# mLSTM scores over all 128 rows, and layer 0's modulation chunks moved off the mLSTM's weights

## The chip, the core and the metric

The kernel runs on one core of a Trainium2 chip. The metric is the device time of one execution in microseconds (us). A core has five engines that run their own instruction streams and wait for each other through semaphores: TensorE (PE; its weight loads are PEld), VectorE (DVE), ScalarE (ACT), GpSimd (POOL) and SyncE (SP), which issues the DMA transfers here.

## What is computed

The reference is a trunk of two layers over 256 latent and 256 context tokens of width 1024, in fp32. Each layer has four mixers side by side, a gated merge, an output projection and an MLP. Two pieces of it matter here. The modulation vector of a layer is a matrix product of one row, which the kernel forms in chunks of weights:

```python
mod = jnp.split((s_c @ w_ada[l] + b_ada[l])[:, None, :], 6, axis=-1)
mod_c = jnp.split(s_cc @ w_ada[l][:, :n_cm * D_MODEL] + b_ada[l][:n_cm * D_MODEL], n_cm)
...
x_l = x_l + mod[2] * (merge_branches((ya_l, yb_l, yc_l, yd_l), lat['gates'], w_branch[l]) @ w_out[l])
```

The mLSTM mixer (B) has 4 heads with keys and queries of 64 columns and values of 128. For each head and each of two directions it computes

```python
s = jnp.einsum('bhtk,bhsk->bhts', qc, kc) * jnp.exp(dmat - m_t[..., None])
num = w_inter[..., None] * jnp.einsum('bhtk,bhkv->bhtv', qc, cmat) + jnp.einsum('bhts,bhsv->bhtv', s, vc)
den = w_inter * jnp.einsum('bhtk,bhk->bht', qc, nvec) + jnp.sum(s, axis=-1)
```

## The kernel before

**Weights.** Every large product is split into a high and a low half of fp32: three products for one. A weight tile is 128x1024 (512 KB). SyncE loads it into one of three `raw` buffers (`_prep`), ScalarE copies its high half `whi` (L139), VectorE subtracts to get the low half `wlo` (L140), and TensorE then runs 24 products of 512 columns with it. Weights are prepared one ahead of use. `plan` writes the list of loads (`specs`) in the order of use; `get` takes the next.

**Modulation chunks.** `plan` puts one chunk of `w_ada` behind each planned weight as long as the list `fill` has any. For layer 0 the list has four halves of eight chunks (`ada_specs`, groups g1 and g2, halves 0 and 1). A chunk is 128x1024, goes through the same `raw` buffers and costs two VectorE updates of an accumulator `aacc` (`ada_chunk`, L390 for a half's first chunk and L392 for the others), one for the latent and one for the context vector. When a half is complete, `ada_sum` sums it over the partitions: eight TensorE products with 32 columns of weights (L404) into a tile of the pool `pm`, a ScalarE copy to a row tile `arow` of the pool `d2` (L407), two transposes (L263) and two VectorE additions into `mod` (L414). `ada_chunk` notes from which use on the sum may be made (`pending`); `get` makes it when that point is reached.

**Order of the work.** A string of units sets in which order the program is written; for layer 0 it is "A RA B b b M0 b b b b b b M0 M0 CD M0 RB C ...". A and RA are the first mixer and its readout; B is the mLSTM's projections (kv, bk, bq, bv: 12 weights) and state; each b is one mLSTM head (four context heads, then four latent ones); each M0 is a quarter of the merge of the first mixer (two gate weights, one branch weight); CD the projections of the two attentions; RB the mLSTM's readout (bo: 4 weights); C the attention. A scheduler then orders the instructions of each engine, in which the heads fall between the products of the weights. Accumulators of weights come from the pool `pd` (4 tiles), those of everything else on TensorE from `pm` (4). A merge quarter's two gate tiles in `pd` are read by two tanh on ScalarE (L1231), which go to `d2` tiles (3).

**A head** (`mixer_b`, from L867). Its scores are two fp32 products of 64 rows and 256 columns (L873). Then for each of the two directions: a product that broadcasts a row of maxima (L878), two VectorE sums with limits (L884, L887), an exponential on ScalarE (L889), two VectorE products with the scores (L890, L891), for latent heads the decayed query `qw` (memset L896, exponential L897, product L898), and five products with the values and the state (L908). At the end the denominator (L912 to L914) and the normalised sum (L917 on ScalarE, L918 on VectorE).

Of the kernel before, what the change touches and what calls it, by code (L numbers as in the profile page):

```python
# [10 lines left out]
AF = mybir.ActivationFunctionType  # L11
# [7 lines left out]
KT = DM // 128  # L19
# [21 lines left out]
class Trunk:  # L41
# [53 lines left out]
    def plan(self, key, parts, split=True, dest=None, fill=True):  # L95
        self.specs.append((key, parts, split, dest))
        if fill and split and self.fill:
            self.specs.append(self.fill.pop(0))

    def wide(self):  # L100

# [268 lines left out]
    def ada_specs(self, l, g):  # L370
        w = self.io["w_ada"]
        out = []
        for k in range(KT):
            for j in range(2):
                c0 = g * 2048 + j * 1024
                out.append((("ada", l, g, k, j), [(w[l, k * 128:(k + 1) * 128, c0:c0 + 1024].rearrange("p (a c) -> p a c", a=1), (1, 1024))], False, None))
        return sorted(out, key=lambda o: o[0][4])

    def ada_chunk(self, key):

        nc = self.nc
        _, l, g, k, jj = key
        raw, _ = self.get(key)
        sides = (0, 1) if l == 0 or g == 0 else (0,)
        if k == 0:
            self.ada_acc = [self.t("w4", [128, 1024], name=f"aacc{g}{jj}{r}") for r in sides]
        for r in sides:
            acc, s = self.ada_acc[r], self.scol[:, k, r:r + 1]
            if k == 0:
                nc.vector.tensor_scalar(out=acc, in0=raw, scalar1=s, scalar2=None, op0=ALU.mult)  # L390
            else:
                nc.vector.scalar_tensor_tensor(out=acc, in0=raw, scalar=s, in1=acc, op0=ALU.mult, op1=ALU.add)  # L392
        if k == KT - 1:
            self.pending = (l, g, jj, sides, self.ada_acc, self.next_use + 1)

    def ada_sum(self, now=False):
        nc = self.nc
# [362 lines left out]
    def mixer_b(self, l):  # L760
        nc = self.nc
# [3 lines left out]
        sides = ((0, 0), (1, CTX)) if need else ((1, CTX),)  # L765
# [26 lines left out]
        for a in range(2):  # L792
            o = a * 256
# [28 lines left out]
        kT = [self.conv(l, 1, mt, self.fm(self.get(("bk", l, mt)), 0, TOK), 0, 0.125) for mt in range(2)]  # L822
        qT = [self.conv(l, 0, mt, self.fm(self.get(("bq", l, mt)), q0, TOK), q0, 1.0) for mt in range(2)]
# [43 lines left out]
        for (sd, t0) in sides:  # L867
            for h in range(HEADS):
                pns = []
                mt, p0 = h // 2, (h % 2) * 64  # L870
                pS = self.pm()
                for st in range(2):
                    nc.tensor.matmul(pS[:, st * 256:(st + 1) * 256], kT[mt][p0:p0 + 64, t0 + st * 128:t0 + (st + 1) * 128],  # L873
                                     qT[mt][p0:p0 + 64, t0:t0 + 256], start=True, stop=True, skip_group_check=True)
                for d in range(2):
                    row = d * 32 + h
                    pM = self.pm()
                    nc.tensor.matmul(pM[:, 0:256], self.rsel[0:100, row:row + 1].to_broadcast([100, 128]), nM[0:100, t0:t0 + 256],  # L878
                                     start=True, stop=True)
                    E = self.t("w2", [128, 512])[:, 0:384]  # L880
                    full = d
                    part = 1 - d
                    tile_of = lambda st: 2 * sd + st
                    nc.vector.scalar_tensor_tensor(out=E[:, 0:256], in0=pM[:, 0:256], scalar=U[:, tile_of(full), row:row + 1],  # L884
                                                   in1=self.mfull[d], op0=ALU.add, op1=ALU.min)
                    pt = slice(128, 256) if d == 0 else slice(0, 128)
                    nc.vector.scalar_tensor_tensor(out=E[:, 256:384], in0=pM[:, pt], scalar=U[:, tile_of(part), row:row + 1],  # L887
                                                   in1=(self.mskf if d == 0 else self.mskb), op0=ALU.add, op1=ALU.min)
                    nc.scalar.activation(out=E, in_=E, func=AF.Exp)  # L889
                    nc.vector.tensor_tensor(out=E[:, 0:256], in0=E[:, 0:256], in1=pS[:, full * 256:(full + 1) * 256], op=ALU.mult)  # L890
                    nc.vector.tensor_tensor(out=E[:, 256:384], in0=E[:, 256:384],  # L891
                                            in1=pS[:, part * 256 + pt.start:part * 256 + pt.stop], op=ALU.mult)
                    if sd:

                        qw = self.t("w2", [128, 512])[:, 0:256]
                        nc.gpsimd.memset(qw[64 - p0:128 - p0], 0.0)  # L896
                        nc.scalar.activation(out=qw[p0:p0 + 64], in_=pM[p0:p0 + 64, 0:256], func=AF.Exp, bias=ME[p0:p0 + 64, 1, row:row + 1])  # L897
                        nc.vector.tensor_tensor(out=qw[p0:p0 + 64], in0=qw[p0:p0 + 64], in1=qT[mt][p0:p0 + 64, t0:t0 + 256], op=ALU.mult)  # L898
                    pn = self.pm()
                    for tt in range(2):  # L900
                        o = pn[:, tt * 129:(tt + 1) * 129]
                        srcs = [(E[:, tt * 128:(tt + 1) * 128], V[:, tile_of(full), h, :])]
                        if tt == (1 if d == 0 else 0):
                            srcs.append((E[:, 256:384], V[:, tile_of(part), h, :]))
                        if sd:
                            srcs.append((qw[:, tt * 128:(tt + 1) * 128], C[:, d, mt, :]))
                        for n, (a, b) in enumerate(srcs):
                            nc.tensor.matmul(o, a, b, start=(n == 0), stop=(n == len(srcs) - 1), skip_group_check=True)  # L908
                    pns.append(pn)
                den = self.sm([128, 2, 2], "bden", 4)  # L910
                for d in range(2):
                    nc.scalar.activation(out=den[:, d, :], in_=pns[d][:, 0:258].rearrange("p (a b) -> p a b", a=2)[:, :, 128], func=AF.Abs)  # L912
                nc.vector.tensor_tensor(out=den, in0=den, in1=EM[:, 2 * sd:2 * sd + 2, :].rearrange("p a b -> p b a")[:, h:h + 33:32, :], op=ALU.max)
                nc.vector.reciprocal(out=den, in_=den)  # L914
                for tt in range(2):
                    o = H[:, 2 * sd + tt, h * 128:(h + 1) * 128]
                    nc.scalar.activation(out=o, in_=pns[0][:, tt * 129:tt * 129 + 128], func=AF.Copy, scale=den[:, 0, tt:tt + 1])  # L917
                    nc.vector.scalar_tensor_tensor(out=o, in0=pns[1][:, tt * 129:tt * 129 + 128], scalar=den[:, 1, tt:tt + 1], in1=o,  # L918
                                                   op0=ALU.mult, op1=ALU.add)
                yield  # L920
# [114 lines left out]
    def mixer_c(self, l):  # L1035
        nc = self.nc
        need = l == 0
        i0 = 0 if need else 2
        q0 = i0 * 128
        KVD, QS, R = self.KVD, self.QS, self.CDR  # L1040
        kn = self.t("w2", [128, 4, 128], name=f"ckn{l}")
        for i in range(4):
            kv = kn[:, i, :].rearrange("p (h c) -> p h c", h=2)
# [323 lines left out]
    def run(self):  # L1367
        nc = self.nc
        for l in range(2):
            if l == 0:  # L1370
                self.plan_start()
                self.fill += self.ada_specs(0, 1) + self.ada_specs(0, 2)
            m = [0] * 4
            for u in ORDER[l].split():
                if u == "A":
                    self.plan_a(l)
                elif u == "RA":
                    self.plan_tmw(("ag", l), l, O_AG)
                elif u == "B":
                    self.plan_b(l)  # L1380
                elif u == "CD":
                    self.plan_cd(l)
                elif u == "RB":
                    self.plan_tmw(("bo", l), l, O_BO)
                elif u[0] == "M":
                    r = int(u[1])
                    self.plan_merge(l, r, (m[r],))
                    m[r] += 1
            self.plan_out(l)
            if l == 0:  # L1390
                self.fill += self.ada_specs(1, 0) + self.ada_specs(1, 1) + self.ada_specs(1, 2)
            self.plan_ff(l)
# [60 lines left out]
        for i in range(2):  # L1453
            for h in range(2):
                o = self.ot[i][:, h * 512:(h + 1) * 512]
# [73 lines left out]
```

## Time and profile before

| | us |
|---|---|
| median of 3 runs | 1815.01 (1813.83 to 1816.32) |
| the profiled execution, its own time | 1811.02 |
| its span, first to last instruction | 1809.2 |
| TensorE busy | 1766.8 |
| VectorE busy | 1201.0 |
| ScalarE busy | 834.5 |
| GpSimd busy | 121.6 |

The profile is one execution. Busy times are sums of instructions; matmuls are pipelined, so the start-to-start step of two products is what each costs in a row, and the printed duration of one is longer than that. Times in the rows below are counted from the start of the span.

### The profile page before, as it was taken

The page shows a single profiled execution, that of the slowest core. Times are in us where ns is not written, and L with a number is a line of the kernel's source. Part 1 is how long each engine was busy: PE and PEld are TensorE (multiplying, and loading weights), DVE is VectorE, ACT ScalarE, POOL GpSimd, SP SyncE. Part 2 cuts the span into 40 slices and gives each one's busy share as a digit, 9 for nine tenths or more (in the row PEclk, how much of TensorE's full clock was granted, in tenths as well). Part 3 has the DMA queues.
Part 4 walks back from the last instruction along what each step waited for, and adds up shares of the span by engine and source line. Part 5 has one row for each costly group of instructions (what it writes and reads, how often), then busy time and mean ns, then how long its engine had stood idle before and what let it go on. Part 6 is the DMA issues. An engine that isn't in the chain of part 4 may idle for free.

```text
span 1809.2 us, 26349 instructions
## 1 busy us (share of the span) xinstructions
PE 1766.8 (98%) x10214; PEld 1494.7 (83%) x10214; DVE 1201.0 (66%) x2047; ACT 834.5 (46%) x1481; POOL 121.6 (7%) x139
## 2 busy tenths in 40 slices
PE   7999989999999999999999999999999999999998
PEld 5788867888677778898888888888789779989998
DVE  5798998657744435489884435587666965656665
ACT  4443533455753334343333334443465664545555
POOL 0000000000011101020101010000000001001110
PEclk9999999999999999999999999999999999999999
DMA  9643345232022234337783334222345425445554
GB/s 294 204 122 102 115 143 162 68 103 84 30 59 70 70 128 128 94 129 222 260 274 93 93 94 140 77 73 57 94 118 179 129 70 162 147 134 164 185 180 137
DMA packets 210045, 234.71 MB, mean 130 GB/s; under 512 B 8320, under 2 KB 186880, under 8 KB 209664
## 3 DMA queue, kind: packets, MB, share of 16 engines
q1 hardware_dynamic: 209920, 233.03, 42.7%
q8 instruction: 80, 1.31, 0.3%
q14 instruction: 45, 0.37, 0.1%
HBM read 228.80 MB, written 4.19 MB: 129 GB/s over the span
## 4 chain that ended last, share of the span: by engine, by line
PE 86%; DVE 6%; ACT 3%; DMA 2%; issue 2%; SPq 0%; POOL 0%; ACTq 0%; DVEq 0%; POOLq 0%
PE pd L198 15%; PE pd L196 15%; PE pd L197 15%; PE pd L168 4%; PE pd L167 4%; PE pd L169 4%; PE pd L238 4%; PE pd L240 4%; PE pd L239 4%; PE pm L263 3%; PE pm L636 2%; DVE wlo L140 2%; PE pm L908 1%; PE pm L1094 1%; DMA raw<-in_w_in_dram 1%
## 5 line engine op out<-in xcount | busy, mean ns | idle before, releaser
L140 DVE TENSOR_TENSOR wlo<-raw,whi 128x1024 fp32r<-128x1024 f32 (+1 forms) x305 | 384.7, 1261 | 278.5 <-ACT whi L139 276.5
L139 ACT ACTIVATE whi<-raw 128x1024 fp32r<-128x1024 f32 (+1 forms) x305 | 321.7, 1056 | 407.4 <-PE pd L197 184.3
L198 PE MATMUL pd<-HH,wlo 128*128 128x256 f32 (+1 forms) x1104 | 371.5, 337 | 2.0 <-DVE wlo L140 1.8
L196 PE MATMUL pd<-HH,whi 128*128 128x256 f32 (+1 forms) x1104 | 372.4, 337 | 0.0
L197 PE MATMUL pd<-HL,whi 128*128 128x256 f32 (+1 forms) x1104 | 370.5, 336 | 0.0
L198 PEld LDWEIGHTS pd<-HH,wlo 128*128 128x128 f32 x1104 | 209.5, 190 | 24.3 <-DVE wlo L140 4.0
L196 PEld LDWEIGHTS pd<-HH,whi 128*128 128x128 f32 x1104 | 209.8, 190 | 21.9 <-issue 1.5
L197 PEld LDWEIGHTS pd<-HL,whi 128*128 128x128 f32 x1104 | 209.8, 190 | 20.3 <-issue 0.5
L196 PE MATMUL pd<-b,whi 128*128 128x256 f32 (+1 forms) x528 | 175.8, 333 | 0.0
L198 PE MATMUL pd<-b,wlo 128*128 128x256 f32 (+1 forms) x528 | 175.4, 332 | 0.2 <-DVE wlo L140 0.2
L197 PE MATMUL pd<-b,whi 128*128 128x256 f32 (+1 forms) x528 | 175.6, 333 | 0.0
L196 PEld LDWEIGHTS pd<-b,whi 128*128 128x128 f32 x528 | 100.4, 190 | 10.5 <-issue 0.8
L198 PEld LDWEIGHTS pd<-b,wlo 128*128 128x128 f32 x528 | 100.4, 190 | 10.2 <-DVE wlo L140 1.0
L238 PE MATMUL pd<-whi,HH 128*128 128x512 f32 (+1 forms) x272 | 106.9, 394 | 1.3 <-ACT whi L139 1.0
L197 PEld LDWEIGHTS pd<-b,whi 128*128 128x128 f32 x528 | 100.4, 190 | 9.4 <-DVE b L1355 0.2
L239 PE MATMUL pd<-whi,HL 128*128 128x512 f32 (+1 forms) x272 | 106.0, 390 | 0.0
L240 PE MATMUL pd<-wlo,HH 128*128 128x512 f32 (+1 forms) x272 | 105.0, 390 | 0.0
L169 PE MATMUL pd<-HH,wlo 128*128 128x512 f32 (+1 forms) x232 | 88.9, 383 | 7.2 <-DVE wlo L140 7.2
L434 ACT ACTIVATE w<-X 128x256 f32<-128x256 f32 x120 | 47.5, 412 | 104.7 <-DVE X L1251 104.7
L1244 POOL TENSOR_TENSOR mg<-mg,d 128x512 f32<-128x512 f32 (+1 forms) x48 | 53.1, 1108 | 555.7 <-DVE d L1243 540.8
L1354 POOL TENSOR_TENSOR d<-d 128x256 f32<-128x256 f32 (+1 forms) x60 | 56.0, 938 | 492.0 <-ACT b L1352 477.1
L168 PE MATMUL pd<-HL,whi 128*128 128x512 f32 (+1 forms) x232 | 89.0, 384 | 0.0
(425 smaller groups left out, 3302.8 us busy)
## 6 DMA issues: line engine op xcount, KB each, us to landing
raw<-in_w_in_dram SPq DMA_DIRECT2D x140, 512.0 KB, 3.7
raw<-in_w_ff_dram SPq DMA_DIRECT2D x128, 512.0 KB, 3.6
w<-in_w_ada_dram SPq DMA_DIRECT2D x48, 512.0 KB, 4.9
raw<-in_w_ada_dram SPq DMA_DIRECT2D x32, 512.0 KB, 3.8
raw<-in_w_branch_dram SPq DMA_DIRECT2D x24, 512.0 KB, 3.5
raw<-in_w_out_dram SPq DMA_DIRECT2D x16, 512.0 KB, 3.5
w<-in_w_ada_dram SPq DMA_DIRECT2D x28, 256.0 KB, 5.6
raw<-in_w_branch_dram SPq DMA_DIRECT2D x16, 256.0 KB, 4.0
```

Source lines behind the costliest of these rows:

```text
L139: nc.scalar.activation(out=hi[:, 0:n], in_=raw[:, 0:n], func=AF.Copy)
L140: nc.vector.tensor_tensor(out=lo[:, 0:n], in0=raw[:, 0:n], in1=hi[:, 0:n].bitcast(F32), op=ALU.subtract)
L167: nc.tensor.matmul(out, lh, rh, start=(i == 0), stop=False)
L168: nc.tensor.matmul(out, lh, rl, start=False, stop=False)
L169: nc.tensor.matmul(out, ll, rh, start=False, stop=(i == n - 1))
L196: nc.tensor.matmul(o, wh, act[0], start=(k == 0), stop=False, skip_group_check=True)
L197: nc.tensor.matmul(o, wh, act[1], start=False, stop=False, skip_group_check=True)
L198: nc.tensor.matmul(o, wl, act[0], start=False, stop=(k == KT - 1), skip_group_check=True)
L238: nc.tensor.matmul(o, hh, wh, start=(k == 0), stop=False, skip_group_check=True)
L239: nc.tensor.matmul(o, hl, wh, start=False, stop=False, skip_group_check=True)
L240: nc.tensor.matmul(o, hh, wl, start=False, stop=(k == KT - 1), skip_group_check=True)
L1354: eng.tensor_tensor(out=r, in0=r, in1=r, op=ALU.mult)
```

## The change

1. A head's scores take the queries from a new tile `qz` of 128 rows, the head's 64 rows copied by ScalarE and the other 64 zeroed by GpSimd, so that the two products have 128 rows (both heads of the key tile stand in the other operand).
2. While B's weights are planned, `fill` is empty: no chunk stands behind them. For layer 0 the list of chunks has an empty entry after each half, so that one weight between two halves has none. The same 32 chunks are used; the last twelve fall behind later weights, up to the last weight of RB.
3. The sum of a half of layer 0 may be made one use earlier (`next_use + l`), and is made at the latest before the next half's first chunk and at the start of the attention C. For layer 1 the number is as before; there, too, the sum now comes at the latest with the next half's first chunk.

```diff
     def plan(self, key, parts, split=True, dest=None, fill=True):
         self.specs.append((key, parts, split, dest))
         if fill and split and self.fill:
-            self.specs.append(self.fill.pop(0))
+            spec = self.fill.pop(0)
+            if spec is not None:
+                self.specs.append(spec)
...
-        return sorted(out, key=lambda o: o[0][4])
+        out = sorted(out, key=lambda o: o[0][4])
+
+        return out if l else out[0:KT] + [None] + out[KT:] + [None]
...
         if k == 0:
+            self.ada_sum(True)
...
-            self.pending = (l, g, jj, sides, self.ada_acc, self.next_use + 1)
+            self.pending = (l, g, jj, sides, self.ada_acc, self.next_use + l)
...
+                qz = self.t("w2", [128, 512])[:, 0:256]
+                nc.gpsimd.memset(qz[64 - p0:128 - p0], 0.0)
+                nc.scalar.activation(out=qz[p0:p0 + 64], in_=qT[mt][p0:p0 + 64, t0:t0 + 256], func=AF.Copy)
                 pS = self.pm()
                 for st in range(2):
-                    nc.tensor.matmul(pS[:, st * 256:(st + 1) * 256], kT[mt][p0:p0 + 64, t0 + st * 128:t0 + (st + 1) * 128],
-                                     qT[mt][p0:p0 + 64, t0:t0 + 256], start=True, stop=True, skip_group_check=True)
+                    nc.tensor.matmul(pS[:, st * 256:(st + 1) * 256], kT[mt][:, t0 + st * 128:t0 + (st + 1) * 128],
+                                     qz, start=True, stop=True, skip_group_check=True)
...
         KVD, QS, R = self.KVD, self.QS, self.CDR
+        self.ada_sum(True)
...
                 elif u == "B":
+
+                    keep, self.fill = self.fill, []
                     self.plan_b(l)
+                    self.fill = keep
```

The scheduler gives another order, too. Line numbers of the changed kernel are larger by 2 to 10: L882 there is the score product (L873 before), L887 the broadcast (L878), L898 and L906 the exponentials (L889, L897), L917 the products with values and state (L908), L921 and L926 the denominator and the normalised half (L912, L917), L409, L412 and L265 the sum, its row and the transposes (L404, L407, L263), L1241 the tanh (L1231), L198 a gate product (L196), L142 a low half (L140), L397 a chunk's update (L392). `pm_...`, `pd_...` and `w2_...` are tiles of the pools.

On TensorE, from the end of the second latent head's products to the third head's in the changed kernel:

```order
L917 MATMUL pm_307_2581<-C0_2197,w2_306_2577 128x129
L882 MATMUL pm_310_2599<-w2_309_2596,w2_218_1960 128x256
L887 MATMUL pm_311_2602<-nM0_1883,rsel_101 128x256
L917 MATMUL pm_314_2614<-bv0_2062,w2_312_2604 128x129
L887 MATMUL pm_315_2620<-nM0_1883,rsel_101 128x256
L917 MATMUL pm_314_2614<-C0_2197,w2_313_2610 128x129
```

The next head's broadcast and its first direction's products follow at once. The same place before, after the second direction of a latent head:

```order
L908 MATMUL pm_311_2651<-C0_2285,w2_310_2647 128x129
L873 MATMUL pm_313_2666<-w2_229_2092,w2_223_2006 128x256
L878 MATMUL pm_314_2669<-nM0_1905,rsel_101 128x256
L198 MATMUL pd_340_2875<-HH_125,wlo87_2881 128x512
L196 MATMUL pd_340_2875<-HH_125,whi87_2880 128x512
L197 MATMUL pd_340_2875<-HL_126,whi87_2880 128x512
```

Here products of a gate weight (`wlo87`, `whi87`) follow the broadcast; seven of them and then twelve of the next weight stand before the head's first direction goes on. In the changed kernel none stands from the second latent head's first direction to the end of the fourth head.

On TensorE of the changed kernel, where those heads end (`aacc110` and `aacc111` are a half's two accumulators, `arow011` its row, `whi71` a gate weight of the third merge quarter):

```order
L917 MATMUL pm_329_2683<-C0_2197,w2_328_2679 128x129
L409 MATMUL pm_333_2734<-aacc110_1539,selr_97 32x256 x3
L409 MATMUL pm_333_2734<-aacc111_1540,selr_97 32x256 x4
L265 MATMUL pm_335_2745<-cst_75,arow011_2743 128x128 x2
L198 MATMUL pd_342_2824<-HH_125,whi71_2788 128x512
```

The sum's products and the transposes of its row stand ahead of the next weight's products.

On ScalarE of the changed kernel at the same place (`d2_336` and `d2_337` are the tanh of the gate tiles of the second merge quarter):

```order
L906 ACTIVATE w2_328_2679<-pm_326_2671,bME_227_2048 64x256
L921 ACTIVATE bden_330_2689<-pm_325_2665 128x2
L921 ACTIVATE bden_330_2689<-pm_329_2683 128x2
L412 ACTIVATE arow011_2743<-pm_333_2734 128x256
L1241 ACTIVATE d2_336_2780<-pd_331_2698 128x512
L1241 ACTIVATE d2_337_2782<-pd_332_2699 128x512
L926 ACTIVATE bh0_2224<-pm_325_2665,bden_330_2689 128x128 x2
```

And before, around one of the same quarter's two tanh (`d2_341`):

```order
L139 ACTIVATE whi88_2912<-raw88_2910 128x1024
L889 ACTIVATE w2_305_2623<-w2_305_2623 128x384
L897 ACTIVATE w2_306_2629<-pm_304_2621,bME_232_2102 64x256
L1231 ACTIVATE d2_341_2940<-pd_339_2874 128x512
L889 ACTIVATE w2_309_2641<-w2_309_2641 128x384
L897 ACTIVATE w2_310_2647<-pm_308_2639,bME_232_2102 64x256
```

The tanh stood between the exponentials of a head; now they stand behind the row of the sum, which stands behind the last head's exponentials.

On VectorE of the changed kernel, between the low halves of two of RB's weights (98 and 100), where the attention's queries `qs0` are prepared:

```order
L142 TENSOR_TENSOR wlo98_3433<-raw98_3430,whi98_3432 128x1024
L397 SCALAR_TENSOR_TENSOR aacc211_3163<-raw99_3462,scol_112,aacc211_3163 128x1024
L1064 TENSOR_TENSOR qs0_2936<-qs0_2936,cdr_382_3270 128x512 x2
L1066 TENSOR_TENSOR qs0_2936<-qs0_2936,gain_651 128x512
L939 TENSOR_TENSOR w2_412_3616<-qs0_2936,rt_659 128x16x16
L142 TENSOR_TENSOR wlo100_3467<-raw100_3464,whi100_3466 128x1024
```

And before, between low halves 99 and 100:

```order
L140 TENSOR_TENSOR wlo99_3407<-raw99_3404,whi99_3406 128x1024
L1056 TENSOR_TENSOR qs0_2996<-qs0_2996,gain_651 128x512
L930 TENSOR_TENSOR w2_404_3592<-qs0_2996,rt_659 128x16x16 x2
L932 TENSOR_TENSOR w2_403_3591<-qs0_2996,rt_659 128x512
L1054 TENSOR_TENSOR qs0_2996<-qs0_2996,cdr_377_3292 128x512
L933 TENSOR_TENSOR w2_403_3591<-w2_403_3591,w2_404_3592 128x512
L930 TENSOR_TENSOR w2_406_3600<-qs0_2996,rt_659 128x16x16
L1060 COPY qs0_2996<-w2_403_3591 128x512
L930 TENSOR_TENSOR w2_406_3600<-qs0_2996,rt_659 128x16x16
L932 TENSOR_TENSOR w2_405_3599<-qs0_2996,rt_659 128x512
L140 TENSOR_TENSOR wlo100_3437<-raw100_3434,whi100_3436 128x1024
```

Chunk updates now share this stretch with the preparation of the attention.

## Rows read from the trace of the kernel before

**Rows 1.** The page's busy times: us, share of the span, number of instructions.

```profile
PE 1766.8 (98%) x10214; PEld 1494.7 (83%) x10214; DVE 1201.0 (66%) x2047; ACT 834.5 (46%) x1481; POOL 121.6 (7%) x139
```

**Rows 2.** Windows: length, busy us (instructions) by engine, granted TensorE clock, DMA share, GB/s.

```profile
220.00:240.00 20.00, 17.14 (x86) 12.88 (x85) 18.01 (x29) 11.24 (x14) 0.00 (x0) 1.00 0.51 152
240.00:260.00 20.00, 17.22 (x70) 13.33 (x69) 18.40 (x27) 7.11 (x12) 0.00 (x0) 0.91 0.40 109
260.00:280.00 20.00, 19.65 (x101) 15.23 (x99) 16.54 (x22) 6.57 (x9) 0.00 (x0) 1.00 0.77 238
...
380.00:400.00 20.00, 20.00 (x135) 18.50 (x134) 9.05 (x14) 13.32 (x31) 0.00 (x0) 1.00 0.27 80
400.00:410.00 10.00, 10.00 (x46) 8.29 (x45) 10.00 (x27) 3.13 (x4) 0.00 (x0) 1.00 0.38 105
410.00:420.00 10.00, 10.00 (x46) 8.29 (x45) 9.05 (x23) 2.12 (x2) 0.00 (x0) 1.00 0.38 107
420.00:430.00 10.00, 10.00 (x47) 8.21 (x46) 4.28 (x5) 3.23 (x5) 0.00 (x0) 1.00 0.36 105
```

**Rows 3.** TensorE's waits, 205 to 282 us: total us, times, longest.

```profile
PE pd L169 <- DVE wlo L140: 4.6, 2, 2.9
```

**Rows 4.** Groups of VectorE lines, 205 to 282 us: busy us, mean ns | idle before.

```profile
L392 DVE SCALAR_TENSOR_TENSOR aacc<-raw,scol,aacc 128x1024 f32<-128x1024 f32 x19 | 23.9, 1274 | 0.0
L140 DVE TENSOR_TENSOR wlo<-raw,whi 128x1024 fp32r<-128x1024 f32 (+1 forms) x12 | 14.4, 1200 | 4.9 <-ACT whi L139 4.8
```

**Rows 5.** Timeline of TensorE, latent heads and attention: start us, us, instruction, records.

```profile
340.45 0.61 PE L908 MATMUL pm<-bv,w 128*128 128x129 f32 x4
...
340.99 0.70 PE L873 MATMUL pm<-w,w 64*128 64x256 f32 x2
...
348.57 0.61 PE L908 MATMUL pm<-bv,w 128*128 128x129 f32 x4
349.02 0.39 PE L908 MATMUL pm<-C,w 128*128 128x129 f32 x2
...
352.07 1.13 PE L873 MATMUL pm<-w,w 64*128 64x256 f32 x4
353.13 0.39 PE L878 MATMUL pm<-nM,rsel 100*128 100x256 f32 x1
...
609.03 2.64 PE L1198 MATMUL pm<-w,vd 128*128 128x256 f32 x11
```

**Rows 6.** Timeline of all engines, one latent head, columns as in rows 5.

```profile
343.11 0.38 PE L878 MATMUL pm<-nM,rsel 100*128 100x256 f32 x1
...
343.33 0.39 PE L198 MATMUL pd<-HH,wlo 128*128 128x512 f32 x1
...
343.56 0.40 PE L196 MATMUL pd<-HH,whi 128*128 128x512 f32 x1
...
344.45 0.34 DVE L887 SCALAR_TENSOR_TENSOR w<-pm,U,cst 128x128 f32<-128x128 f32 x1
...
345.87 0.51 ACT L889 ACTIVATE w<-w 128x384 f32<-128x384 f32 x1
...
347.14 0.41 DVE L890 TENSOR_TENSOR w<-w,pm 128x256 f32<-128x256 f32 x1
...
347.67 0.41 DVE L898 TENSOR_TENSOR w<-w,w 64x256 f32<-64x256 f32 x1
...
348.00 0.67 DVE L1241 SCALAR_TENSOR_TENSOR mg<-d,pd 128x512 f32<-128x512 f32 x1
...
348.60 0.47 DVE L884 SCALAR_TENSOR_TENSOR w<-pm,U,cst 128x256 f32<-128x256 f32 x1
```

**Rows 7.** Timeline of TensorE, the sum of a half, columns as in rows 5.

```profile
275.18 1.07 PE L404 MATMUL pm<-aacc,selr 128*32 128x256 f32 x16
```

**Rows 8.** Windows of a later gap, layer 1, columns as in rows 2.

```profile
1608.00:1612.00 4.00, 1.41 (x8) 1.02 (x6) 2.13 (x6) 2.13 (x4) 0.00 (x0) 0.87 0.00 1
1612.00:1616.00 4.00, 2.81 (x12) 2.26 (x11) 4.00 (x10) 2.21 (x6) 0.00 (x0) 0.50 0.42 131
```

## The prediction

> **What bounds the kernel now.** Line numbers here are those of the kernel before. I read the busy shares first. TensorE is busy for 98% of the span [rows 1], so an edit counts only where it opens or closes a TensorE gap. Next come the windows of the stretch that the change touches [rows 2]. Inside the mLSTM's projections (220 to 280 us) TensorE lacks 2.86, 2.78 and 0.35 us of three times 20 us, 6.0 in all, while VectorE is busy for 18.0, 18.4 and 16.5. The waits name the cause: L169 waits for `wlo`, the low half of a weight that VectorE makes [rows 3]. The groups of VectorE lines in that stretch show whose work stands ahead of it: 19 chunk updates (L392) of 1.274 us beside 12 splits (L140) of 1.200 [rows 4]. The granted clock's mean is 0.91 from 240 to 260 us [rows 2], which costs another 0.09 times 20 = 1.8 us. From 380 us on TensorE has no gap, though VectorE is full from 400 to 410 [rows 2].
>
> **Scores over 128 rows.** The four records of a head's two score products start at 352.07 and the next instruction at 353.13: 1.06 us [rows 5]. A 128-row fp32 product of the same 256 columns (L1198) has eleven records in 2.64 us, the last lasting about 0.4: 0.22 each, so 0.88 for four. Entering is dear as well: four L908 records take 0.54 us when L873 follows (340.45 to 340.99) and 0.45 when it doesn't (348.57 to 349.02). So 0.27 us per group in a row. The 48 records of the 12 heads stand in 17 such groups, since in five heads another product parts them: 4.6 us, with bounds 0 (if the padded form still pays the entry and the step) and 5. I take 4.6, because L1198 differs from the new form in its operands alone. The added zero fill is on GpSimd and needs no product's result; the added copy on ScalarE reads the finished queries. Both can run ahead of the head that needs them, and weight products cover them: nothing. Uncovered, a copy of 64 rows costs ScalarE no more than L889 with 384 columns, 0.51.
>
> The Trainium skill, "TensorE: Matmul & The Clock Gate", section "Why this matters for your kernels", says that a single matmul over few rows takes the same time as one over all 128. By that rule this edit gives back nothing and my sum is 4.6 us too low. The rows speak against it, 0.27 against 0.22 per record. "TensorEngine Tiling (Array Packing)" of the Trainium skill, section "Key Properties", has a changed tiling mode drain the array, which agrees with the dearer entry.
>
> **Chunks out of the mLSTM's projections.** Twelve chunks of two updates leave: 24 times 1.274 = 30.6 us of VectorE work, from a stretch where it worked 53 of 60 us. The splits then come on time. Gone are most of the 6.0 us of gaps and the 1.8 of half clock; the rest of VectorE's serial work on the gates stays, and so does the wait for ScalarE's high half (L238 there). I take 7.2, bounds 5 and 8. SyncE loses every second transfer in this stretch, and the freed prefetch slots hold weights, so loading is no worse.
>
> **What comes late instead.** The chunks now end with the readout's weights, 15 specs later than before. From 380 to 430 us VectorE worked 9.05 + 10.00 + 9.05 + 4.28 = 32.4 of 50 us [rows 2]. TensorE takes 24 products of 0.23 = 5.5 us per weight (343.33 to 343.56) [rows 6], so about nine chunks land there: 9 times 2.55 = 23 us, in all 55. That is 5 us more than TensorE's time. The three raw buffers let chunks lag and the following weights run freely, so part is absorbed: I take 4, bounds 0 and 8.
>
> **The sum's new place.** This is the term that decides. In the order of the changed kernel the last three latent heads of the mLSTM stand on TensorE with no weight product between them: the last seven products of one weight (whi69), then some 45 rows of head products, then the sum of a half (L404) and its two transposes, then whi71. Before, weight products stood between the two directions of each of these heads. The reason is on ScalarE: `arow` (L407) now comes ahead of the two tanh (L1231) that read the finished gate tiles, since the sum is taken at the free step, ahead of the tanh in the program; before, the tanh stood between the heads. Until those tanh have run, whi71 has no accumulator to write (four in the pool). So whi71 waits for `arow`, `arow` for the sum, and the sum stands behind the heads. ScalarE holds the last L917 and the next high halves behind `arow`; VectorE holds the merge's multiplies (L1241) and the next chunks, and SyncE their slots.
>
> How long do three bare heads take? One head, from L878 to the next L878, was 343.11 to 353.13 = 10.0 us [rows 5, 6]. Foreign work in it: L889 had its input at 344.45 + 0.34 = 344.79 and began at 345.87, behind a weight's high half (1.1 lost). L890 began at 347.14, though L889 ended at 346.38, behind a split (0.75). The second direction's L884 began at 348.60, though L898 ended at 348.08, behind the merge's L1241 (0.5). With 0.2 for the scores, 7.5 us remain. In the new order the first head still has a high half and a split in it (9.0), the next are bare (7.5 each). The third also has two reductions for the norm between its halves, 1.1 together (an estimate: the 512 columns of L1241, 0.67, at most twice). Behind it stand the sum (1.0 for its 16 records), `arow` and one tanh (no longer than L889's 0.51 each, nearly) and three handovers of about 0.2, together some 2.6, an estimate. Sum: 9.0 + 7.5 + 7.5 + 1.1 + 2.6 = 27.7 us.
>
> TensorE's own work in it: seven weight products (1.6); a head's scores (0.88), two L878 (0.44) and 20 records of L908 at 0.11 (2.2), so 3.5 us for each of two heads and 2.4 for the first, which is under way; the sum 1.0 [rows 7]. That makes 12.0. Idle: 27.7 - 12.0 = 15.7; I take 14, since some of the handovers will overlap. Upper bound: heads as slow as before, 3 times 10.0 + 3.7 - 12.0 = 22. Lower bound: one direction (348.60 to 353.13, 4.5) wholly beside the other, so three heads of 4.5 and 1.1 + 2.6, less 12.0: 5.
>
> **The clock in it.** Where TensorE was busy 1.41 of 4 us (1608 to 1612) the clock was 0.87, and in the next 4 us 0.50 [rows 8]. In the new stretch TensorE is busy for half of 27 us. At half clock a head's chain grows by its own products (L878, L908, scores, at least 2.2 + 0.4 us again), 7.8 for three, and a half-clock 4 us behind it costs 2: at most 10, at least 0. I take 4.
>
> The layer 1 sums come a weight earlier beside TensorE work that covers them: nothing.
>
> **The sum.** The profiled execution has a span of 1809.2 and a time of 1811.02; the median of the three runs is 1815.01, 0.2% above. I apply the change to the median: -4.6 - 7.2 + 4 + 14 + 4 = +10.2, 1825.
>
> **The rivals.**
> 1. *The gap is short and the gains win* (faster). One mechanism: the two directions of each bare head overlap, as ScalarE and VectorE are no longer shared with weights. Then idle is 5, the clock 0, the late chunks 2: -11.8 + 7 = -4.8, 1810. It decides below 8.2 us of new loss in all (gains of 11.8 less 3.6). For it: one direction of a head takes 4.5 us of the 7.5. Against it: in the order the second L878 of a head stands behind the first direction's first L908, so they can overlap little. 0.13.
> 2. *Gains and gap cancel* (within 0.2%): idle 10 without half clock, late chunks 2: -11.8 + 12, 1815. For it: whether half clock is granted depends on where the products fall. 0.17.
> 3. *All of it bad*: idle 17 at half clock all through, late chunks 7: -11.8 + 17 + 9 + 7 = +21, 1836. 0.17.
> 4. *The scores change does nothing*: the forecast with 0 for 4.6 saved, 1830. Its rows are against it; 0.10, inside the range.
>
> My forecast has the remaining 0.43. 0.2%, 3.6 us, is about what a measurement of this kernel can tell from no change. Slower by more: 0.43 + 0.17 + 0.10 = 0.70. Within: 0.17. Faster: 0.13. The range, 1812 to 1838, takes in the third rival and the second, and leaves out most of the first and a tail above.
>
> **What would show it.** TensorE at 20.00 of 20 in windows over the mLSTM's projections, with no half clock, would confirm the 7.2. Score steps of 0.22 would confirm the 4.6. Between the last product of whi69 and the first of whi71 I expect about 27 us, with TensorE waiting for `w` tiles from VectorE (L890, L898) and at the end for `arow` and the tanh. VectorE near full while the readout's weights run, and waits for `wlo` there, would confirm the 4. I am wrong if that stretch is under 20 us, or if whi71's products start before the sum.

## The result, and the profile after

The changed kernel takes 1826.97 us (median of 4 runs, 1824.94 to 1829.74) against 1814.42 for the kernel before (4 runs): 12.5 us more, a ratio of 1.0067 with a 95% interval of 1.0055 to 1.0080, which is 10.0 to 14.5 us. The forecast was 1825. The profiled execution took 1827.39 us.

The page of the changed kernel, its busy times and the engines' shares of the chain that ended last (the first line answers to [rows 1]):

```profile
PE 1770.8 (97%) x10214; PEld 1498.6 (82%) x10214; DVE 1203.3 (66%) x2047; ACT 840.4 (46%) x1493; POOL 126.3 (7%) x151
...
PE 83%; DVE 8%; DMA 4%; ACT 3%; issue 2%; SPq 0%; ACTq 0%; DVEq 0%
```

Every engine is busy for what it was before, within 6 us; most of the loss is not work but waiting and a slower clock. The windows of the changed kernel say where (columns as in [rows 2]; its mLSTM heads lie between 273 and 351 us):

```profile
220.00:240.00 20.00, 18.01 (x81) 14.45 (x80) 16.41 (x31) 11.35 (x14) 0.00 (x0) 1.00 0.24 69
240.00:260.00 20.00, 19.17 (x86) 15.48 (x86) 12.66 (x19) 8.28 (x13) 0.31 (x1) 1.00 0.37 106
260.00:280.00 20.00, 19.89 (x114) 15.86 (x113) 13.78 (x21) 7.26 (x14) 0.30 (x1) 1.00 0.53 158
...
320.00:340.00 20.00, 13.05 (x56) 11.07 (x54) 11.74 (x33) 7.49 (x20) 1.53 (x5) 0.74 0.09 27
340.00:360.00 20.00, 16.85 (x79) 12.07 (x79) 14.41 (x28) 8.62 (x20) 0.00 (x0) 0.83 0.35 103
...
400.00:420.00 20.00, 18.20 (x90) 15.10 (x89) 16.46 (x21) 12.29 (x30) 0.00 (x0) 1.00 0.44 136
...
440.00:460.00 20.00, 18.08 (x97) 13.65 (x95) 15.79 (x33) 11.15 (x18) 0.00 (x0) 0.91 0.26 77
```

The last of these windows in the kernel before:

```profile
440.00:460.00 20.00, 19.78 (x112) 14.29 (x110) 15.72 (x40) 14.69 (x39) 1.39 (x1) 1.00 0.17 54
```

Three things are to be seen. In the first three windows TensorE lacks 1.99, 0.83 and 0.11 us where it lacked 2.86, 2.78 and 0.35 [rows 2], and the clock is 1.00 where its mean was 0.91: a gain of 3.1 + 1.8 = 4.9. From 320 to 360 us it lacks 6.95 + 3.15 = 10.1 us and the clock is at 0.74 and 0.83. From 400 to 460, where the readout's weights and the attention's start now share VectorE with chunks, TensorE lacks 1.80 and 1.92, and the clock is 0.91 at the end.

The timeline of the changed kernel over its last three latent heads (start us, us, instruction; L171 is the last product of whi69, L887 the broadcast that begins a head, L917 the products with the values, L409 the sum, L412 arow, L1241 the tanh, L198 the first product of whi71):

```profile
318.75 0.47 PE L887 MATMUL pm<-nM,rsel 100*128 100x256 f32 x1
...
320.44 0.39 PE L171 MATMUL pd<-ya,wlo 128*128 128x512 f32 x1
323.44 0.77 PE L917 MATMUL pm<-bv,w 128*128 128x129 f32 x2 [2.60 <-DVE w L899]
...
327.84 0.64 PE L917 MATMUL pm<-bv,w 128*128 128x129 f32 x2
328.26 0.64 PE L917 MATMUL pm<-C,w 128*128 128x129 f32 x2
...
329.96 0.47 PE L887 MATMUL pm<-nM,rsel 100*128 100x256 f32 x1
...
332.91 0.46 PE L917 MATMUL pm<-bv,w 128*128 128x129 f32 x2 [2.48 <-DVE w L899]
...
336.77 0.39 PE L917 MATMUL pm<-bv,w 128*128 128x129 f32 x2
336.99 0.39 PE L917 MATMUL pm<-C,w 128*128 128x129 f32 x2
...
337.91 0.47 PE L887 MATMUL pm<-nM,rsel 100*128 100x256 f32 x1
...
348.06 1.93 PE L409 MATMUL pm<-aacc,selr 128*32 128x256 f32 x14
...
350.04 0.38 ACT L412 ACTIVATE arow<-pm 128x256 f32<-128x256 f32 x1 [1.71 <-PE pm L409]
...
350.32 1.08 ACT L1241 ACTIVATE d<-pd 128x512 f32<-128x512 f32 x2
...
350.97 0.53 PE L198 MATMUL pd<-HH,whi 128*128 128x512 f32 x1
```

From the last product of whi69 to the first of whi71 pass 30.5 us, and nothing but heads and the sum runs on TensorE between them. Most of TensorE's idle time there is a wait for the exponentials that VectorE has multiplied with the scores (320 to 352 us: total us, times, longest):

```profile
PE pm L917 <- DVE w L899: 9.5, 5, 2.9
```

The order of the end is the one that the prediction read: the sum, arow 1.7 us after ScalarE began to wait for it, then both tanh, and whi71 0.65 us after the first of them began.

### The profile page after: what moved, and what is told of

The parts are those of the page before. It is cut to its first block, busy times and chain, and to the rows that moved or that the text cites. A ratio compares the mean times of both kernels' runs of the same rounds, so it can differ in the third digit from the quotient of the medians.

```text
span 1825.6 us, 26415 instructions
## 1 busy us (share of the span) xinstructions
PE 1770.8 (97%) x10214; PEld 1498.6 (82%) x10214; DVE 1203.3 (66%) x2047; ACT 840.4 (46%) x1493; POOL 126.3 (7%) x151
## 4 chain that ended last, share of the span: by engine, by line
PE 83%; DVE 8%; DMA 4%; ACT 3%; issue 2%; SPq 0%; ACTq 0%; DVEq 0%
PE pd L200 14%; PE pd L198 14%; PE pd L199 14%; PE pd L240 4%; PE pd L170 4%; PE pd L169 4%; PE pd L242 4%; PE pd L171 4%; PE pd L241 4%; PE pm L265 2%; PE pm L641 2%; DVE wlo L142 2%; DMA raw<-in_w_ada_dram 2%; PE pm L917 2%; PE pm L1104 1%
## 5 line engine op out<-in xcount | busy, mean ns | idle before, releaser
L142 DVE TENSOR_TENSOR wlo<-raw,whi 128x1024 fp32r<-128x1024 f32 (+1 forms) x305 | 385.7, 1265 | 265.1 <-ACT whi L141 263.1
L198 PE MATMUL pd<-HH,whi 128*128 128x256 f32 (+1 forms) x1104 | 372.9, 338 | 0.1
L198 PEld LDWEIGHTS pd<-HH,whi 128*128 128x128 f32 x1104 | 209.9, 190 | 22.6 <-issue 1.2
L198 PE MATMUL pd<-b,whi 128*128 128x256 f32 (+1 forms) x528 | 175.6, 333 | 0.0
L198 PEld LDWEIGHTS pd<-b,whi 128*128 128x128 f32 x528 | 100.3, 190 | 10.5 <-issue 0.8
L171 PE MATMUL pd<-HH,wlo 128*128 128x512 f32 (+1 forms) x232 | 87.5, 377 | 5.4 <-DVE wlo L142 5.4
```

The lines of the kernel that those rows point to most:

```text
L142: nc.vector.tensor_tensor(out=lo[:, 0:n], in0=raw[:, 0:n], in1=hi[:, 0:n].bitcast(F32), op=ALU.subtract)
L171: nc.tensor.matmul(out, ll, rh, start=False, stop=(i == n - 1))
L198: nc.tensor.matmul(o, wh, act[0], start=(k == 0), stop=False, skip_group_check=True)
```

## The experiments

All times are medians, each against the kernel before on the same chip; where two experiments are compared, their differences to their own before are. The first four take the change apart.

**The scores alone** (`e1_scores`): the kernel before with this part of the change and no other.

```diff
+                qz = self.t("w2", [128, 512])[:, 0:256]
+                nc.gpsimd.memset(qz[64 - p0:128 - p0], 0.0)
+                nc.scalar.activation(out=qz[p0:p0 + 64], in_=qT[mt][p0:p0 + 64, t0:t0 + 256], func=AF.Copy)
...
-                    nc.tensor.matmul(pS[:, st * 256:(st + 1) * 256], kT[mt][p0:p0 + 64, t0 + st * 128:t0 + (st + 1) * 128],
-                                     qT[mt][p0:p0 + 64, t0:t0 + 256], start=True, stop=True, skip_group_check=True)
+                    nc.tensor.matmul(pS[:, st * 256:(st + 1) * 256], kT[mt][:, t0 + st * 128:t0 + (st + 1) * 128],
+                                     qz, start=True, stop=True, skip_group_check=True)
```

> The kernel before with the 128-row scores alone. The prediction's term: 17 groups of score records at 0.27 us saved each, so 4.6 us faster than before (about 1810 against 1814.4). Rival (few rows cost what all rows cost, or the added copy stands in the head's chain): no faster than before, 1814 or more.

Measured: 1806.47 against 1813.82, ratio 0.9961 (0.9948 to 0.9974), so 7.4 us faster, 4.7 to 9.4. The rival has fallen: rows that are padded with zeros do pay here. The timeline of this kernel's TensorE shows where (L877 the scores, L882 the broadcast, L169 a weight's product):

```profile
340.07 0.60 PE L877 MATMUL pm<-w,w 128*128 128x256 f32 x2
340.32 0.47 PE L882 MATMUL pm<-nM,rsel 100*128 100x256 f32 x1
...
349.33 1.03 PE L877 MATMUL pm<-w,w 128*128 128x256 f32 x4
350.01 0.47 PE L882 MATMUL pm<-nM,rsel 100*128 100x256 f32 x1
350.32 0.40 PE L169 MATMUL pd<-ya,wlo 128*128 128x512 f32 x1
```

Four records begin at 349.33 and the broadcast at 350.01: 0.68 us, where it was 1.06 (352.07 to 353.13 in [rows 5]) and the prediction had 0.88. Three steps are 0.22 each, as foreseen; the fourth is next to nothing, since the broadcast begins right behind the start of the last score product. Part of it comes back: the broadcast's own step to the next weight product is 0.31 instead of 0.22 (343.11 to 343.33 in [rows 6]).

A group of two tells what the 64 rows cost. Before, it and the step to the broadcast at 343.11 [rows 6] took 0.63 us:

```profile
342.48 0.70 PE L873 MATMUL pm<-w,w 64*128 64x256 f32 x2
```

Now they take 0.25 (340.07 to 340.32). In both forms two more products cost 0.43, so one costs 0.22 with 64 rows and with 128; what is saved lies at the ends of a group, 0.38 whether it has two products or four. With the entry, 0.09 as forecast, and the 0.09 that come back, 17 groups make 6.5 us. That lies inside the measured interval, as a gain of 4.7 would.

**The chunk part alone** (`e2_chunks`): the changed kernel with the scores of before.

```diff
-                qz = self.t("w2", [128, 512])[:, 0:256]
-                nc.gpsimd.memset(qz[64 - p0:128 - p0], 0.0)
-                nc.scalar.activation(out=qz[p0:p0 + 64], in_=qT[mt][p0:p0 + 64, t0:t0 + 256], func=AF.Copy)
...
-                                     qz, start=True, stop=True, skip_group_check=True)
+                                     qT[mt][p0:p0 + 64, t0:t0 + 256], start=True, stop=True, skip_group_check=True)
```

> The changed kernel with the scores of before (64 rows), so the chunk part alone. If the two parts add up: 4.6 us slower than the changed kernel, about 1831.5, with the same bare heads on TensorE. Rival (the copy into qz stands in the bare heads' chain and costs what the scores save): equal to the changed kernel, 1827.

Measured: 1834.49 against 1813.82, 1.0117 (1.0102 to 1.0132): 20.7 us slower. It and the scores' -7.4 make 13.3, beside 12.5 for both together, so the parts add up within the scatter, and no cost of the copy into `qz` in bare heads can be seen.

**The sum one use later** (`e3_later`), as in the kernel before; all else as changed. In its order the tanh stand between the heads again, and so do the products of whi71 and whi73.

```diff
-            self.pending = (l, g, jj, sides, self.ada_acc, self.next_use + l)
+            self.pending = (l, g, jj, sides, self.ada_acc, self.next_use + 1)
```

> The changed kernel, but the sum of a layer 0 half one use later (next_use + 1 as before, all else changed). Sum theory: arow now comes behind the two tanh on ScalarE, whi71 can start, the heads lie between weight products again and about 18 us (14 idle and 4 of clock) come back: 1809, below before. Rival (VectorE's load from chunks among the heads and later is the cost): chunks stand where they stood, so about 1825 to 1827.

Measured: 1816.9 against 1813.82, 1.0018 (1.0008 to 1.0028). Of 12.5 us 9.5 have come back, so the rival of VectorE's load is out as the main cause, but not the 18 that were expected. **A buffer of its own for arow** (`e4_arow`), with the sum where the change puts it, does the same from the other end:

```diff
-        self.bufs = {"w2": 10, "d2": 3, "p2": 2, "w4": 4, "w8": 4, "b16": 3}
+        self.bufs = {"w2": 10, "d2": 3, "p2": 2, "w4": 4, "w8": 4, "b16": 3, "ar": 1}
...
-            row = self.t("d2", [128, 512], name=f"arow{l}{g}{jj}")[:, 0:256]
+            row = self.t("ar", [128, 256], name=f"arow{l}{g}{jj}")
```

> The changed kernel, but arow in a buffer of its own rather than in the pool that the tanh share; the sum stays at its place in the program. Sum theory in its narrow form (the shared pool orders arow ahead of the tanh): as with the later sum, about 1809. Rival (the sum's products, queued behind the heads, hold TensorE themselves): still about 1827. Rival of VectorE's load: 1827.

Measured: 1814.75 against 1813.82, 1.0004 (0.9995 to 1.0014), so 11.6 of the 12.5 have come back. The row tile's place in the pool it shared with the tanh is what set the order on ScalarE: with a buffer of its own the three heads lie between weight products, and the sum stands where it stood. On ScalarE the second tanh now comes ahead of arow:

```profile
338.94 0.60 ACT L1241 ACTIVATE d<-pd 128x512 f32<-128x512 f32 x1 [0.30 <-PE pd L200]
...
343.75 0.38 ACT L412 ACTIVATE arow<-pm 128x256 f32<-128x256 f32 x1 [0.84 <-PE pm L409]
```

What is left in both is a second gap. Of `e4_arow` the window:

```profile
340.00:360.00 20.00, 15.38 (x69) 11.13 (x70) 17.66 (x26) 7.23 (x16) 0.00 (x0) 0.83 0.60 188
```

Of `e3_later` the window, TensorE's longest wait in 340 to 360 us (total us, times, longest) and SyncE's in 320 to 352:

```profile
340.00:360.00 20.00, 14.74 (x68) 10.46 (x67) 16.25 (x26) 8.65 (x19) 0.00 (x0) 0.83 0.51 160
```

```profile
PE pd L169 <- ACT whi L141: 3.5, 1, 3.5
```

```profile
SPq L126 <- DVE bden L922: 21.1, 1, 21.1
```

Behind the sum TensorE waits 3.5 us for the high half of the next weight, and before that SyncE had stood for 21.1 us without issuing a transfer. The first chunk of the next half can't be taken up while its accumulators have no buffer (the pool `w4` has four: two old accumulators until the sum has read them, the mLSTM's state C, and one), and untaken chunks hold the `raw` buffers. In the changed kernel SyncE stood for 25.6 us in the same way:

```profile
SPq L126 <- DVE bden L922: 25.6, 1, 25.6
```

There no gap behind the sum shows, probably because the weights already loaded were not used up during the bare heads; that was not tested.

**Two tests of where a half ends.** The first moves the chunks and does nothing else: no free step, no earlier sum, 64-row scores (`e5_skip_only`).

```diff
                 elif u == "B":
+                    keep, self.fill = self.fill, []
                     self.plan_b(l)
+                    self.fill = keep
```

> The kernel before (64-row scores, sum and list of chunks as before), but no chunks behind the mLSTM's weights. Its order, too, has arow ahead of the second merge quarter's tanh and three bare heads. Sum theory: what decides is where a half ends, not the free step nor the earlier sum; like the chunk part alone, about 20 us slower than before, 1834. Rival (the free step or the earlier sum brings the loss): near before, 1810 to 1818.

Measured: 1833.1 against 1814.27, 1.0108 (1.0093 to 1.0123), 18.8 us slower. The second is its counterpart, the changed kernel with chunks behind the mLSTM's weights (`e6_no_skip`):

```diff
                 elif u == "B":
-
-                    keep, self.fill = self.fill, []
                     self.plan_b(l)
-                    self.fill = keep
```

> The changed kernel with chunks behind the mLSTM's weights again: 128-row scores, free step and earlier sum stay. No bare heads in its order. Sum theory: like the scores alone, 1806 to 1808. Rival (free step and earlier sum cost by themselves): 1815 or more.

Measured: 1808.26 against 1814.27, 0.9967 (0.9954 to 0.9980), which can't be told from the scores alone. So the free step and the earlier sum cost nothing by themselves that can be seen. Moving twelve chunks puts the sum of a half between the two gate weights of the second merge quarter, with the free step (the half ends there) and without it (the half ends one use before), and that brings the loss.

**Four or eight chunks instead of twelve.** Both have the 128-row scores, the list and the sum of before, and leave out chunks behind the first four (`c1_skip4`) or the first eight (`c1_skip8`) of the mLSTM's weights.

```diff
     def plan_b(self, l):
+        keep, self.fill = self.fill, []
         self.plan_tmw(("kv", l), l, O_KV0, w=464)
+        self.fill = keep
         for nm, o in (("bk", O_BK), ("bq", O_BQ)):
             for mt in range(2):
                 self.plan((nm, l, mt), [self.win(l, o + 128 * mt, 128)])
...
         self.plan_tmw(("bv", l), l, O_BV)
```

(for eight, the second added line stands below the loop)

> 128-row scores, and no chunks behind the first four of the mLSTM's twelve weights only; no free step, sum as before. Four chunks move late. A half then ends at the second merge quarter's gates: arow ahead of the tanh and three bare heads. Sum theory: the whole 18 us of that place over the scores alone (1806.5), less little gained, 1823 to 1826. Rival (cost goes by the number of chunks moved late): a third of the chunk part's 20.7, so 1813.

> 128-row scores, and no chunks behind the first eight of the mLSTM's twelve weights; no free step, sum as before. Eight chunks move late, but the half ends elsewhere and the order has weight products between all heads. Sum theory: no bare heads; gain of about 3 in the projections against late chunks of about 3, so 1805 to 1809. Rival (by the number of chunks): two thirds of 20.7, so 1820.

Measured: 1827.45 (1.0073, 1.0051 to 1.0094) with four, 1808.54 (0.9972, 0.9962 to 0.9981) with eight. This is the sharpest of the tests. With four, a half ends behind the first merge quarter, and its sum falls between the second quarter's gate weights again; with eight it falls a quarter later, behind the last head. Moving four chunks costs 20.5 us over the scores alone (+13.2 against -7.4), moving eight costs 1.6. The windows of the one with four, then of the one with eight:

```profile
320.00:340.00 20.00, 14.67 (x80) 12.07 (x78) 11.44 (x37) 8.15 (x24) 2.44 (x8) 0.91 0.01 2
340.00:360.00 20.00, 13.67 (x58) 9.27 (x59) 14.32 (x27) 9.11 (x20) 0.00 (x0) 0.74 0.39 116
```

```profile
320.00:340.00 20.00, 20.00 (x109) 16.67 (x108) 14.29 (x36) 9.86 (x23) 2.37 (x8) 1.00 0.20 61
340.00:360.00 20.00, 18.10 (x111) 14.52 (x109) 16.52 (x40) 9.52 (x24) 0.61 (x2) 1.00 0.25 75
360.00:380.00 20.00, 19.40 (x83) 16.05 (x84) 16.04 (x16) 8.49 (x14) 0.00 (x0) 0.91 0.78 241
```

With four, TensorE lacks 11.7 us in two windows and the clock falls to 0.91 and 0.74, as in the changed kernel. With eight the heads are covered, and what is left is a gap of 1.90 + 0.60 us at the end of them, with the clock at 0.91 behind it.

**The accumulators' buffer.** A buffer of its own for the state C frees one of the pool `w4` (three small pools are one buffer smaller to make room), first with the later sum (`e9_later_cown`), then with eight chunks moved (`c2_skip8_cown`), then as a control with the scores alone (`c3_scores_cown`).

```diff
-        C = self.t("w4", [128, 2, 2, 129], name=f"C{l}")
+        C = self.t("cs", [128, 2, 2, 129], name=f"C{l}")
```

> The changed kernel with the sum one use later (as e3_later) and a buffer of its own for the mLSTM's state C, so that the next half's accumulators find one in their pool without waiting for the sum. If SyncE's 21.1 us wait and TensorE's 3.7 us gap behind the sum in e3_later (with 3 us of half clock) come from chunks that hold raw buffers: 5 to 7 us faster than e3_later's 1816.9, 1810 to 1812. Rival (the gap comes from the transfers or ScalarE's order): unchanged, 1817.

> c1_skip8 with a buffer of its own for C. Its gap of 2.7 us behind the sum and the half clock of the window behind it should go: 3 to 4 us faster than 1808.5, 1805. If the held raw buffers are not its cause: 1808.5.

> The kernel before with 128-row scores and C in a buffer of its own, the control for the two others: no gap behind a sum to remove, so as the scores alone, 1806.5 (1805 to 1808). If the extra buffer helps in itself: 1803 or less.

Measured: 1809.74 (0.9980, 0.9971 to 0.9989), 1803.81 (0.9950, 0.9933 to 0.9966) and 1808.27 (0.9970, 0.9959 to 0.9981), each against 1813.54. The second gap was the held buffers: 6.9 us come back from `e3_later`, 4.0 from `c1_skip8`, and nothing in the control (5.3 faster than before, beside 7.4 for the scores alone). The windows with the later sum, then two with eight chunks:

```profile
340.00:360.00 20.00, 18.12 (x104) 14.02 (x103) 18.56 (x37) 9.69 (x25) 0.61 (x2) 1.00 0.36 106
```

```profile
340.00:360.00 20.00, 20.00 (x122) 16.62 (x121) 19.14 (x45) 10.33 (x25) 0.61 (x2) 1.00 0.43 129
360.00:380.00 20.00, 20.00 (x118) 17.81 (x117) 11.15 (x14) 8.37 (x14) 0.00 (x0) 1.00 0.64 197
```

In the first the clock is 1.00 where it was 0.83 in `e3_later`, and in the second no gap is left. `c2_skip8_cown` is faster than both kernels of the change: 128-row scores, eight chunks moved, and the half's end and the buffers placed so that nothing waits for the sum. Its lead over `e1_scores`, 2.4 us, lies inside the overlap of the two intervals. The control is the nearer comparison, with the same buffers and against the same before: there the lead is 4.5 us, and the slowest of its four runs (1805.78) is below the fastest of the control's seven (1807.07). So moving eight chunks gains something where nothing waits for the sum; moving twelve, in `e9_later_cown`, gains nothing over the control.

## Why the prediction was right

The sign and the place were forecast, and about 20 us of loss lie where 18 were put. That the total came within 2.3 us owes something to luck: the scores gave more than forecast, the projections less. The terms one by one, those below the scores read from one execution of each kernel:

| term | forecast | shown |
|---|---|---|
| scores | -4.6 | -7.4 (-9.4 to -4.7), `e1_scores`; -6.5 by the steps |
| projections without chunks | -7.2 | -4.9, windows 220 to 280 |
| bare heads and sum, idle | +14 | +10.1, windows 320 to 360 |
| half clock in them | +4 | +10.1, what is left of 32.2 |
| late chunks | +4 | about +5, windows 400 to 460 |
| sum | +10.2 | +12.5 (10.0 to 14.5) measured; the column adds up to 12.9 |

**Scores.** The sign and the entry were right, the size was about 2 us too small by the steps. The term priced the last product of a group like the others; behind a 128-row product the broadcast starts at once. The row for L1198 could have told: it was read up to its eleventh product [rows 5]; a twelfth follows, and the next instruction starts at 611.53, so that twelve take 2.50 us and not twelve times 0.22. The prediction's 0.27 against 0.22 per record is a mean over the group; inside a group the 64-row step is 0.22 too.

The Trainium skill, "TensorE: Matmul & The Clock Gate", section "Why this matters for your kernels", says that a single product over few rows takes the same time as one over all. The steps of 0.22 inside a group agree with it. What the prediction drew from it, that the edit gives back nothing, does not follow: the scores alone would have stayed at 1813.8, and 1806.47 was measured.

**Projections.** Here 2.3 us too much was forecast. The chunks were not all that held up the low halves. Where before the wait was 2.86 us, 1.99 is left. The timeline of the changed kernel:

```profile
231.92 0.67 DVE L805 TENSOR_TENSOR_SCAN w<-w 4x256 f32<-4x256 f32 x1
...
232.62 0.68 DVE L806 TENSOR_TENSOR_SCAN w<-w 4x256 f32<-4x256 f32 x1
...
234.66 0.50 PE L171 MATMUL pd<-HH,wlo 128*128 128x512 f32 x1 [1.99 <-DVE wlo L142]
```

VectorE's scans over the gates stand ahead of the split, with no chunk near. They stood there before the change, too:

```profile
234.74 0.68 DVE L801 TENSOR_TENSOR_SCAN w<-w 4x256 f32<-4x256 f32 x1
...
235.52 1.20 DVE L140 TENSOR_TENSOR wlo<-raw,whi 128x1024 fp32r<-128x1024 f32 x1
```

So the longest of the waits was misread: the prediction counted the chunk updates of the whole stretch, but ahead of this split the last of them had begun at 228.14, and work on the gates filled the time from 229.34. The prediction named that serial work as what stays, and put it at 0.6 of 7.8 us.

**Bare heads and sum.** The 27.7 us were added up from the first head's broadcast to the first product of whi71. In the timeline that is 318.75 to 350.97, 32.2 us: 11.2, 8.0 and 10.1 for the three heads, where 9.0, 7.5 and 8.6 were put, and 2.9 behind them, where 2.6 were. (The 30.5 us start with the last of the seven weight products that the prediction counts in.) Less the 12.0 of TensorE's own work at full clock, 20.2 are lost; the forecast was 14 + 4. The split was off: 10.1 idle and as much again in which products took longer than their step at full clock. The granted clock, 0.74 and 0.83, fell short by 0.26 and 0.17 of 20 us each, 8.6 in all, which is the most that it can account for; no run tests this split. The total was tested, by taking the order away: from the changed kernel to `e9_later_cown`, which has the same chunks at the same weights, 16.3 us come back (+12.5 and -3.8). The rival in which the two directions overlap fell with the timeline: a head from broadcast to broadcast took 7.95 us (329.96 to 337.91) and not 4.5, and the first L917 of a head waits about 2.5 us for `w`.

**What the prediction did not see.** The chunks that wait for accumulators and hold the `raw` buffers show no wait of TensorE's in the changed kernel, but kept 7 us of what the later sum could have brought back. The prediction said of SyncE only that its slots are held.

**Late chunks.** TensorE lacks 1.80 us in 400 to 420, waiting for a low half as forecast, and in 440 to 460 it lacks 1.92 against 0.22 before, with the clock at 0.91 (1.8). TensorE's waits from 400 to 450 us in the changed kernel (total us, times, longest):

```profile
PE pm L265 <- DVE bh L728: 1.8, 2, 0.9
PE pd L200 <- DVE wlo L142: 1.8, 1, 1.8
```

The second is the wait that was named, but not for the reason that was named. The prediction had more VectorE work than time; here VectorE stood idle for 2.20 us behind a chunk update whose transfer had not landed, while the high half that the split needs was done at 406.30:

```profile
405.25 1.05 ACT L141 ACTIVATE whi<-raw 128x1024 fp32r<-128x1024 f32 x1
...
406.97 1.29 DVE L397 SCALAR_TENSOR_TENSOR aacc<-raw,scol,aacc 128x1024 f32<-128x1024 f32 x1 [2.20 <-DMA raw<-in_w_ada_dram]
...
408.77 1.22 DVE L142 TENSOR_TENSOR wlo<-raw,whi 128x1024 fp32r<-128x1024 f32 x1
...
410.04 0.50 PE L200 MATMUL pd<-HH,wlo 128*128 128x512 f32 x1 [1.80 <-DVE wlo L142]
```

The first is the readout's transposes, which wait for VectorE too. That all of this is the chunks' doing was read from the traces and not tried alone.

## What to carry to other kernels

Before moving work between steps, look at where its end falls: a small reduction at the end of a block can stand in an order, on a shared pool of row tiles or accumulators, ahead of what another chain needs, and moving four blocks can cost as much as moving twelve. Read the order for stretches in which the busiest engine has only a latency chain, and add up that chain from the trace. When a repair brings back less than the chain, look for the next holder of buffers behind it: here a prefetch queue stood for 21 us behind one accumulator.

## What the runs showed of the hardware

Two fp32 score products follow each other in 0.22 us with 64 rows and with 128. The ends of the group differ: behind a 128-row product the broadcast starts almost at once (four records and the step to the broadcast take 0.68 us, three steps of 0.22), while the same with 64 rows takes 1.06 [rows 5].

The granted clock was 0.74 and 0.83 over the 40 us of the bare heads, in which TensorE counts as busy for 29.9; in the gaps of the projections it had been 0.91 over 20 us [rows 2]. Two records of L917 take 0.42 us there at half clock (327.84 to 328.26) and 0.22 at full (336.77 to 336.99), so that about half of what was lost there is not idle time in any row.
